# The up product of a conv FFN layer: sums of the right operand in place, another order of its seven products

## The chip, the cores and the metric

The kernel runs on one core of one Trainium2 chip, in float32. The metric is the device time of one execution in microseconds (us); of the kernel before there are three runs. Everything below about its inside comes from one profiled execution of it.

## The reference, cut to what matters

One layer of a diffusion transformer: adaptive modulation, a gated linear attention mixer beside a short convolution, the mixer's output product, a residual, and a conv FFN. The change touches the output product, the norm behind it and the FFN's first product (the up product):

```python
x = x + gt1 * rmsnorm(yx @ w_out, g_post_mix)          # 1024 tokens x 1024
hx = modulate(rmsnorm(x, g_pre_ffn), sh2, sc2)
u, gate = split(hx @ w_up, 2, axis=-1)                 # w_up: 1024 x 5632
u = dwconv_grid(u, w_cf, b_cf, 16, 64)                 # 3x3 taps on a grid of 16 x 64 tokens
x = x + gt2 * rmsnorm((silu(u) * gate) @ w_down, g_post_ffn)
```

All results are float32. The FFN has 2816 features, 22 tiles of 128; a pair `p` is one tile of u and the gate tile that belongs to it.

## The kernel before

**Products.** Each float32 operand is split into a high and a low part (`split`, L127 on ScalarE for the high part, L134 mostly on VectorE or GpSimd for the low), and a product is three matmuls: high by high, high by low, low by high (`mm3`, L144 to L146), each 128 x 128 by 128 x 512.

**The up product** is done by a scheme of Strassen's kind. For a pair, its four products of halves (u and gate, tokens 0 to 511 and 512 to 1023, over two halves of the 1024 inputs) become seven products m = 1 to 7. Each is 4 K tiles of 3 matmuls, so 12 matmuls into a PSUM bank of 128 x 512. Its left operand is a block of the pair's weights or a sum of blocks (`up_sum`; the sums run on GpSimd, L1161, into tiles `rs`), split by ScalarE and GpSimd into tiles `p`. Its right operand is a block of the normed tokens or a sum of blocks. Two right operands (tiles `b11` and `d0`) are made token tile by token tile in `norm2`; the others (`mx`) are made by `mixed` after the mixer's output product: sums `ms` over blocks `blk` at L1193, then splits.

**Banks.** The generator `pair` yields the next product, its bank, and whether it accumulates on what stands there. The order is 3, 4, 5, 1, 2, 7, 6 with banks bx, by, bx, bz, by, bz, bw. Where a bank is used twice, VectorE or ScalarE reads the value of the first product out, and the second accumulates on it. VectorE's six reads per pair are L1320, L1323, L1326, L1329, L1331 and L1337 (for the pairs ahead: L1308, L1311, L1315, L1331, L1337). Between the reads VectorE works on the 3x3 taps of the pair before (`conv`, L1260, one operation of 1.2 us per tap) and on sums of the gated features for the down product (L1279 to L1287).

**The pairs ahead.** For pairs 0 to 3 two of the seven products (4 and 2) run early (`early_prep`, `early_dot`): their right operands need only the first half of the tokens, so TensorE does them while the last token tile is normed.

**What sets the order.** TensorE's order is written out in the program throughout. The order on VectorE, ScalarE and GpSimd is that of the program from the transition on (`ordered`); ahead of it, and on SyncE (SP), which issues the loads and stores, a scheduler sets it. At `AHEAD = 3` products ahead, `load_up` and `prep_up` load and split the weights.

**The mixer's output product** runs over eight token tiles c (`w_out`), each with two halves of 512 columns; `half_stats` and `residual` norm a tile's result, and `norm2(c - 1)` transposes the token tile before, on TensorE, into `blk`. Tile 7's `norm2` comes after the early products of pairs 0 and 1. Its inputs are spilled earlier and loaded by SP: `so` (L1015), the gate's activations `sog` (L1018), the token rows x (L1020).

## Time and profile before

| what | value |
|---|---|
| median of 3 runs | 1190.06 us (1187.59 to 1190.59) |
| the profiled execution | 1189.29 us |
| its span | 1187.5 us |
| mean granted clock of TensorE | 0.989 |
| matmuls by the page | 5770, busy 1149.9 us (97%) |
| VectorE / ScalarE / GpSimd busy | 77% / 45% / 43% |

The span is what the profile records from the first to the last instruction. A row of the timeline gives start, duration, engine, line, operation, result<-inputs; in brackets the idle time ahead of the operation and what released it. A row of the groups gives the count, busy time, mean ns of one, and idle time before. A row of the windows gives the length, then busy time and count for TensorE, its weight loads, VectorE, ScalarE and GpSimd, then the granted clock as a share of full speed, the DMA engines' share, and GB/s. The mixing product's end, the transition and the up product lie at about 424 to 524, 524 to 570 and 570 to 985 us; then the down product follows.

### The profile page before, as it was taken

How to read it: one execution, taken by the hardware profiler on the slowest of the kernel's cores; microseconds unless marked ns; L12 is line 12 of the kernel's file. 1: busy time of each engine (PE TensorE's matmuls, PEld its weight loads, DVE VectorE, ACT ScalarE, POOL GpSimd, SP SyncE). 2: the span in 40 equal slices, each digit the busy share in tenths (PEclk: the TensorE clock that was granted, in tenths of full speed). 3: DMA queues.
4: the chain of work that ended last, by engine and by line, in shares of the span. 5: the costliest groups of instructions: out<-in, count | busy, mean ns of one | idle time of the engine just before them, and what ended most of it. 6: DMA issues, size and time to landing. Idle time of an engine off the chain costs nothing.

```text
span 1187.5 us, 15973 instructions
## 1 busy us (share of the span) xinstructions
PE 1149.9 (97%) x5770; PEld 945.9 (80%) x5770; DVE 910.0 (77%) x1237; ACT 531.4 (45%) x945; POOL 506.4 (43%) x415
## 2 busy tenths in 40 slices
PE   8899999979999999997999999999999999999997
PEld 6689977867877888885788888888888888888885
DVE  4965657898779456658689998888888887877676
ACT  5745156634243155555334434343434344544453
POOL 3111001233344201147888888787888872000002
PEclk9999999999999999999999999999999999999999
DMA  9883844401112273232213341233213249977663
GB/s 338 274 306 132 284 147 126 142 28 45 54 36 72 73 248 125 88 107 71 71 63 116 143 142 64 96 124 116 92 69 124 98 155 328 356 248 257 224 222 132
DMA packets 80128, 176.19 MB, mean 148 GB/s; under 512 B 9809, under 2 KB 21585, under 8 KB 80050
## 3 DMA queue, kind: packets, MB, share of 16 engines
q1 hardware_dynamic: 80050, 175.19, 43.7%
q8 instruction: 45, 0.74, 0.3%
q14 instruction: 33, 0.27, 0.1%
HBM read 142.38 MB, written 32.78 MB: 148 GB/s over the span
## 4 chain that ended last, share of the span: by engine, by line
PE 68%; DVE 12%; issue 7%; DMA 6%; POOL 3%; ACT 3%; SPq 0%; DVEq 0%; POOLq 0%; ACTq 0%
PE ps L144 21%; PE ps L146 21%; PE ps L145 21%; DMA ada<-in_ada 4%; DVE ada L229 3%; PE ps L889 2%; DVE su L852 2%; PE ps L334 1%; DVE p L134 1%; POOL rs L1161 1%; POOL ms L1193 1%; PE ps L923 1%; PE ps L922 1%; DVE mx L134 1%; DVE hxl L350 1%
## 5 line engine op out<-in xcount | busy, mean ns | idle before, releaser
L1260 DVE SCALAR_TENSOR_TENSOR y<-u,cols,y 128x945 f32<-128x945 f32 (+2 forms) x176 | 214.9, 1222 | 2.4
L144 PE MATMUL ps<-mx,p 128*128 128x512 f32 x440 | 174.5, 397 | 8.0 <-DVE t L1308 5.5
L145 PE MATMUL ps<-mx,p 128*128 128x512 f32 x440 | 174.6, 397 | 0.0
L146 PE MATMUL ps<-mx,p 128*128 128x512 f32 x440 | 174.2, 396 | 0.0
L134 POOL TENSOR_TENSOR p<-rs,p 128x512 fp32r<-128x512 f32 x106 | 138.2, 1306 | 39.8 <-ACT p L127 39.7
L146 PE MATMUL ps<-p,p 128*128 128x512 f32 x308 | 120.1, 390 | 0.2
L145 PE MATMUL ps<-p,p 128*128 128x512 f32 x308 | 120.1, 390 | 0.0
L144 PE MATMUL ps<-p,p 128*128 128x512 f32 x308 | 119.8, 389 | 0.0
L1161 POOL TENSOR_TENSOR rs<-wr 128x512 f32<-128x512 f32 x77 | 109.6, 1424 | 2.0 <-DMA wr<-in_wu 2.0
L134 POOL TENSOR_TENSOR wl<-wr,wh 128x1024 fp32r<-128x1024 f32 x16 | 41.4, 2593 | 158.9 <-ACT wh L127 158.9
L144 PEld LDWEIGHTS ps<-mx,p 128*128 128x128 f32 x440 | 83.6, 190 | 29.2 <-issue 7.0
L144 PE MATMUL ps<-hxh,wh 128*128 128x512 f32 x256 | 106.6, 416 | 0.0
L229 DVE CUSTOM_DVE_ANT_0 ada<-ada,cb 128x1024 f32<-128x1024 f32 x64 | 80.8, 1277 | 26.0 <-DMA ada<-in_ada 25.6
L146 PE MATMUL ps<-hxh,wl 128*128 128x512 f32 x256 | 100.6, 393 | 0.0
L145 PE MATMUL ps<-hxl,wh 128*128 128x512 f32 x256 | 100.2, 392 | 0.0
L145 PEld LDWEIGHTS ps<-mx,p 128*128 128x128 f32 x440 | 83.5, 190 | 19.1
L146 PEld LDWEIGHTS ps<-mx,p 128*128 128x128 f32 x440 | 83.5, 190 | 19.0
L127 ACT ACTIVATE p<-rs 128x512 fp32r<-128x512 f32 x110 | 68.5, 627 | 33.3 <-POOL rs L1161 32.9
L876 POOL TENSOR_TENSOR ek<-ek,kh 128x1024 f32<-128x1024 f32 x12 | 29.7, 2478 | 92.2 <-ACT ek L127 92.2
L145 PEld LDWEIGHTS ps<-p,p 128*128 128x128 f32 x308 | 57.8, 188 | 12.7 <-DVE p L134 0.7
L146 PEld LDWEIGHTS ps<-p,p 128*128 128x128 f32 x308 | 57.8, 188 | 12.7 <-DVE p L134 0.8
L144 PEld LDWEIGHTS ps<-p,p 128*128 128x128 f32 x308 | 57.8, 188 | 12.0
(282 smaller groups left out, 2678.2 us busy)
## 6 DMA issues: line engine op xcount, KB each, us to landing
ada<-in_ada SPq DMA_DIRECT2D x64, 512.0 KB, 4.5
wr<-in_wu SPq DMA_DIRECT2D x48, 512.0 KB, 4.4
h<-hd SPq DMA_DIRECT2D x77, 256.0 KB, 4.5
hd<-h SPq DMA_DIRECT2D x73, 256.0 KB, 2.1
wdr<-in_wd SPq DMA_DIRECT2D x55, 256.0 KB, 3.6
wdr<-in_wd SPq DMA_DIRECT2D x22, 512.0 KB, 5.9
x<-in_x SPq DMA_DIRECT2D x16, 512.0 KB, 5.1
wr<-in_wb SPq DMA_DIRECT2D x16, 512.0 KB, 3.7
```

The source lines that it names most:

```text
L127: return S.activation(o, i, fn, **kw)
L134: (eng or V).tensor_tensor(lo, raw, hi.bitcast(F32), ALU.subtract)
L144: PE.matmul(ps, lh, rh, start=first, stop=False, skip_group_check=more)
L145: PE.matmul(ps, lh, rl, start=False, stop=False, skip_group_check=more)
L146: PE.matmul(ps, ll, rh, start=False, stop=last, skip_group_check=more)
L229: V.tensor_tensor_reduce(raw, raw, cbs[which], 1.0, 0.0, ALU.mult, ALU.add, dst)
L334: PE.matmul(pt[:, j * P : (j + 1) * P], xs[t][:, ft * P : (ft + 1) * P], dgs[t], start=True, stop=True)
L852: V.scalar_tensor_tensor(slot(n)[lo : lo + DK, hs], slot(c)[lo : lo + DK, hs], dec[lo : lo + DK, h, c : c + 1], slot(n)[lo : lo + DK, hs], ...
L876: G.tensor_tensor(kl, kl, kh[hf], ALU.mult)
L889: PE.matmul(pts[hh][:, o : o + P], kl[r, fb, cs], ql[r, fb, cs], start=True, stop=True)
L1161: G.tensor_tensor(r, src[0], src[1], ALU.add if terms[1] > 0 else ALU.subtract)
L1260: V.scalar_tensor_tensor(y3[:, ro, co], u3[:, ri, ci], col("wcf", 9 * p + 3 * (dr_ + 1) + dc + 1), y3[:, ro, co], ALU.mult, ALU.add)
```

## The change

The right operands' sums are made in place, one token tile at a time. `norm2` returns four VectorE operations (128 x 512 each, L1086 to L1089 of the changed kernel) for a token tile of the second half; they write into `blk` and a tile `t7`. `mixed` now only splits. Rows of the first half make the tiles `b11` and `b21`. Four GpSimd row sums per pair remain of five, since one result serves the next.

The order of products becomes 1, 2, 6, 7, 4, 5, 3 (ahead: 6, 7, 4, 5, 3), with banks bx, by, bx, bz, bz, bw, bw. VectorE reads a bank five times per pair (L1319 or, ahead, L1312, then L1330, L1332, L1335 and L1337), ScalarE twice. The early products are 1 and 2, and tile 7's `norm2` stands between 1 and 2 of pair 1. The last token tile's output product goes K tile by K tile over both halves: five K tiles, then `norm2(6)`, then the rest. The order written out on VectorE, ScalarE and GpSimd begins with the last token tile. gv2 is loaded at the start of the down product, gv1 lies in a buffer of the output weights, and a constant (`tri`) moves to another pool.

```diff
-        b11, d0 = ([ph.tile([P, KQ, 512], F32R, name=f"{n}{i}") for i in range(2)] for n in ("b11", "d0"))
+        b11, b21 = ([ph.tile([P, KQ, 512], F32R, name=f"{n}{i}") for i in range(2)] for n in ("b11", "b21"))
...
+            x11, x12, x21, x22 = (blk[g][h][:, :, cs] for g in range(2) for h in range(2))
             if th == 0:
-                x0, x1 = (blk[g][0][:, :, cs] for g in range(2))
-                split(x0, b11[0][:, :, cs], b11[1][:, :, cs], heng=V)
-                raw = p2.tile([P, KQ, P], F32, tag="fd", bufs=1, name=nm("fd"))
-                fold(d0[0][:, :, cs], d0[1][:, :, cs], raw, x1, -1, x0, V, V, V)
...
+                split(x11, b11[0][:, :, cs], b11[1][:, :, cs], heng=V)
+                split(x21, b21[0][:, :, cs], b21[1][:, :, cs])
             else:
-                w_out(mh, ml, py, (0,), range(8))
-                if c < NT - 1:
-                    mix = mix_prep(c + 1)
-                w_out(mh, ml, py, (1,), range(5))
-                norm2(c - 1, *last)
-                xn, ss = norm_tiles()
-                half_stats(py, 0, xn, ss)
-                w_out(mh, ml, py, (1,), range(5, 8))
-            half_stats(py, 1, xn, ss)
-            normed = residual(c, xt, xn, ss)
-
-
-
-
-
-        pclose("pw")
-        pclose("pvo")
-        pc = popen("pc", "left", bufs=1)
-        py = popen("py", "left", bufs=1)
-
-        h_d = {m: [dr.tile([P, 512], F32, name=f"hd{m}_{i}") for i in range(KH)] for m in range(1, 8)}
-        FACT = {
-            1: (((0, 0), 1, (1, 1)), ((0, 0), 1, (1, 1))),
-            2: (((0, 1), 1, (1, 1)), ((0, 0),)),
-            3: (((0, 0),), ((0, 1), -1, (1, 1))),
-            4: (((1, 1),), ((1, 0), -1, (0, 0))),
-            5: (((0, 0), 1, (1, 0)), ((1, 1),)),
-            6: (((0, 1), -1, (0, 0)), ((0, 0), 1, (0, 1))),
-            7: (((1, 0), -1, (1, 1)), ((1, 0), 1, (1, 1))),
-        }
-
-
-        def up_raw(p, gate_only=False):
-            if gate_only or POS[p] % 2 == 0:
-                r = [None if gate_only and n == 0 else wp.tile([P, KT, P], F32, tag="wraw", name=nm("wr")) for n in range(2)]
+                d = t7[:, :, cs]
+                return [lambda: V.tensor_tensor(d, x22, x12, ALU.subtract),
+                        lambda: V.tensor_tensor(x12, x12, x11, ALU.subtract),
+                        lambda: V.tensor_tensor(x11, x11, d, ALU.add),
+                        lambda: V.tensor_tensor(x21, x21, x11, ALU.subtract)]
...
+        right = {6: blk[0][0], 7: t7, 4: blk[1][0], 5: blk[0][1], 3: blk[1][1]}
+        mixes = {}
+
+        def mixed(m, cols):
+
+            if m not in mixes:
+                mixes[m] = room("mx", pr, tag="mx", bufs=4) if m == 3 else room("mx", pa, tag="a")
+                rhs[m] = lambda kt: tuple(x[kt // 2][:, kt % 2, :] for x in mixes[m])
+            for g in range(2):
+                split(right[m][:, 2 * g : 2 * g + 2, cols], *(x[g][:, :, cols] for x in mixes[m]))
...
+        def up_sum(p, m, raw, free=True):
+            def row_sum(a, b, sign, r=None):
+                if r is None:
+                    r = pc.tile([P, KQ, P], F32, tag="rs", bufs=3, name=nm("rs"))
+                G.tensor_tensor(r, a, b, ALU.add if sign > 0 else ALU.subtract)
+                return r
+
+            a11, a12, a21, a22 = (r[:, KQ * h : KQ * h + KQ, :] for r in (raw[0], raw[-1]) for h in range(2))
+            if m == 6:
+                sums_of[p] = s7 = row_sum(a11, a21, -1)
+                sums_of[p] = s7, row_sum(a22, s7, -1)
+            return free, {1: lambda: a11, 2: lambda: a12, 4: lambda: a22, 5: lambda: row_sum(a21, a22, 1),
+                          6: lambda: sums_of[p][1], 7: lambda: sums_of[p][0],
+                          3: lambda: row_sum(a12, sums_of[p][1], -1, sums_of[p][1])}[m]()
...
+            elif c == NT - 1:
+                w_out(mh, ml, py, (0, 1), range(5))
+                early_prep(0)
+                sums = norm2(c - 1, *last)
+                mixed(6, c2)
+                mixed(7, c2)
+                w_out(mh, ml, py, (0, 1), range(5, 6))
+                w_out(mh, ml, py, (0,), range(6, 8))
+                xn, ss = norm_tiles()
+                half_stats(py, 0, xn, ss)
+                w_out(mh, ml, py, (1,), range(6, 8))
...
-        def mixed(m, hi, lo, cols, stage):
-            terms = FACT[m][1]
-            for g in range(2):
-                src = [blk[kh][th][:, 2 * g : 2 * g + 2, cols] for kh, th in terms[::2]]
-                h, l = hi[g][:, :, cols], lo[g][:, :, cols]
-                raw = src[0]
-                if len(src) > 1:
...
-                    raw = sums_of[m, g][:, :, cols]
-                if stage == 0:
-                    (G if m == 7 or m == 6 and g else V).tensor_tensor(raw, src[0], src[1],
-                                                            ALU.add if terms[1] > 0 else ALU.subtract)
-                elif stage == 1:
-                    split(raw, h, l)
...
-        UP, UP_AHEAD = (3, 4, 5, 1, 2, 7, 6), (3, 1, 5, 7, 6)
+        UP, UP_AHEAD = (1, 2, 6, 7, 4, 5, 3), (6, 7, 4, 5, 3)
...
             bx = bank(ps_mm)
-            yield 3, bx, False
-            if ahead:
-                V.tensor_tensor(t, g1, bx, ALU.add)
-                bz = bank(ps_mm)
-                yield 1, bz, False
-                V.tensor_tensor(g1, t, bz, ALU.add)
-                G.tensor_tensor(g1, g1, g0, ALU.subtract)
-                yield 5, bx, True
+            if p in kept:
+                u = kept[p].rearrange("p a b -> p (a b)")
+                yield 6, bx, False
+                V.tensor_tensor(u[:, hi], u[:, hi], bx, ALU.add)
+            else:
+                yield 1, bx, False
+                u = pc.tile([P, T], F32, tag="u", bufs=2, name=nm("u"))
                 act(u[:, hi], bx)
-                V.tensor_tensor(u[:, lo], t, bx, ALU.subtract)
+                by = bank(ps_mm)
+                yield 2, by, False
+                V.tensor_tensor(u[:, lo], u[:, hi], by, ALU.add)
+                yield 6, bx, True
+                act(u[:, hi], bx)
+            bz = bank(ps_mm)
+            yield 7, bz, False
+            if p == SEQ[-1]:
+                g = py.tile([P, T], F32, tag="y", bufs=3, name=nm("g"))
+            elif POS[p] % 2:
+                g = ph.tile([P, 2, T], F32, tag="blk", bufs=4, name=nm("g"))[:, 0, :]
             else:
-                act(t, bx)
-                by = bank(ps_mm)
-                yield 4, by, False
-                V.tensor_tensor(t, t, by, ALU.add)
-                yield 5, bx, True
-                act(u[:, hi], bx)
-                V.tensor_tensor(u[:, lo], t, bx, ALU.subtract)
-                bz = bank(ps_mm)
-                yield 1, bz, False
-                V.tensor_tensor(g1, t, bz, ALU.add)
-                yield 2, by, True
-                act(g0, by)
-                V.tensor_tensor(g1, g1, by, ALU.subtract)
-            yield 7, bz, True
-            V.tensor_tensor(u[:, lo], u[:, lo], bz, ALU.add)
+                g = pr.tile([P, T], F32, tag="g", bufs=2, name=nm("g"))
+            V.tensor_tensor(g[:, hi], u[:, hi], bz, ALU.add)
+            yield 4, bz, True
+            V.tensor_tensor(g[:, lo], u[:, hi], bz, ALU.add)
+            bw = bank(ps_mm)
+            yield 5, bw, False
+            V.tensor_tensor(g[:, hi], g[:, hi], bw, ALU.add)
+            yield 3, bw, True
+            V.tensor_tensor(u[:, hi], u[:, hi], bw, ALU.add)
             y = pools["yy"][1].tile([P, T], F32, tag="yy", bufs=2, name=nm("y"))
-            later.append(lambda: act(y, u, AF.Identity, bias=col("bcf", p), scale=col("wcf", 9 * p + 4)))
-            started.append(conv(p, u, y, g.rearrange("p a b -> p (a b)")))
-            bw = bank(ps_mm)
-            yield 6, bw, False
-            V.tensor_tensor(g1, g1, bw, ALU.add)
+            act(y, u, AF.Identity, bias=col("bcf", p), scale=col("wcf", 9 * p + 4))
+            started.append(conv(p, u, y, g))
...
-        early_prep(0)
         early_prep(1)
-        mixes = {m: room("mx", pa, tag="a") for m in MIXES[:4]}
-        c3, c1, call = slice(0, 3 * P), slice(3 * P, 4 * P), slice(0, 4 * P)
-        mixed(3, *mixes[3], c3, 0)
+        mixed(4, c2)
+        mixed(6, c6)
+        mixed(7, c6)
+        early_dot(0)
+        early_dot(1, lambda: [f() for f in norm2(NT - 1, *normed)])
+        mixed(6, c1)
         early_prep(2)
-        mixed(5, *mixes[5], c3, 1)
-        mixed(3, *mixes[3], c3, 1)
-        mixed(7, *mixes[7], c3, 0)
-        mixed(1, *mixes[1], c3, 0)
-        early_dot(0)
-        early_dot(1)
-        norm2(NT - 1, *normed)
+        keep(0)
+        mixed(7, c1)
         pclose("p2")
         pr = popen("pr", "right", bufs=1)
-        mixes[6] = room("mx", pr, tag="mx", bufs=4)
-        mixed(3, *mixes[3], c1, 0)
-        mixed(1, *mixes[1], c1, 0)
-        mixed(7, *mixes[7], c1, 0)
-        mixed(3, *mixes[3], c1, 1)
-        keep(0)
         early_prep(3)
-        mixed(1, *mixes[1], call, 1)
         early_dot(2)
+        keep(1)
+        mixed(4, c6)
         early_dot(3)
         load_up(0)
         prep_up(0)
         gen = pair(0)
         step = next(gen)
-        keep(1)
+        mixed(4, c1)
         load_up(1)
         prep_up(1)
-        mixed(5, *mixes[5], c1, 1)
+        mixed(5, slice(0, 512))
         load_up(2)
         prep_up(2)
-        mixed(6, *mixes[6], call, 0)
-        mixed(7, *mixes[7], call, 1)
+        mixed(3, slice(0, 512))
         load_up(3)
...
+        gv2 = pd.tile([P, D], F32, name="gv2")
+        SY.dma_start(gv2, gv2_row)
```

TensorE in a steady pair before: the last matmuls of product 2 and the first of product 7, which accumulates on product 1. In a row `ps` is a PSUM bank, `mx` or `b` the right operand, `p` the weights; brackets hold the semaphores waited for.

```order
L144 MATMUL ps_6003<-b_3825,p_6006 128x512
L145 MATMUL ps_6003<-b_3826,p_6006 128x512
L146 MATMUL ps_6003<-b_3825,p_6006 128x512
L144 MATMUL ps_6049<-mx_4852,p_6027 128x512 [waits DVE_49,Activation_49]
L145 MATMUL ps_6049<-mx_4854,p_6027 128x512
L146 MATMUL ps_6049<-mx_4852,p_6027 128x512 [waits Pool_49]
```

Product 1 lies in ps_6049, and the twelve matmuls of product 2 in ps_6003 stand between it and product 7. After, the end of product 7 and the start of product 4:

```order
L144 MATMUL ps_5986<-mx_4704,p_5907 128x512
L145 MATMUL ps_5986<-mx_4706,p_5907 128x512
L146 MATMUL ps_5986<-mx_4704,p_5907 128x512
L144 MATMUL ps_5986<-mx_4844,p_5948 128x512 [waits DVE_49]
L145 MATMUL ps_5986<-mx_4846,p_5948 128x512
L146 MATMUL ps_5986<-mx_4844,p_5948 128x512 [waits Pool_49]
```

Product 4 follows in the same bank ps_5986 as product 7, and its first matmul waits for VectorE. The same holds where 3 follows 5:

```order
L144 MATMUL ps_6033<-mx_5044,p_5967 128x512
L145 MATMUL ps_6033<-mx_5046,p_5967 128x512
L146 MATMUL ps_6033<-mx_5044,p_5967 128x512
L144 MATMUL ps_6033<-mx_5054,p_5991 128x512 [waits DVE_49,Activation_49]
L145 MATMUL ps_6033<-mx_5056,p_5991 128x512
L146 MATMUL ps_6033<-mx_5054,p_5991 128x512 [waits Pool_49]
```

VectorE over a steady pair before, from the read of product 4 to that of product 7:

```order
L1320 TENSOR_TENSOR t_5712<-t_5712,ps_5735 128x512
L1267 TENSOR_TENSOR h_5774<-y_5577,g_5443 128x1024
L1260 SCALAR_TENSOR_TENSOR y_5687<-u_5603,cols,y_5687 128x16x63
L1323 TENSOR_TENSOR u_5713<-t_5712,ps_5714 128x512
L1260 SCALAR_TENSOR_TENSOR y_5687<-u_5603,cols,y_5687 128x16x63
L1326 TENSOR_TENSOR g_5711<-t_5712,ps_5781 128x512
L1279 TENSOR_TENSOR h_5622<-h_5622 128x512
L1260 SCALAR_TENSOR_TENSOR y_5687<-u_5603,cols,y_5687 128x15x63
L1329 TENSOR_TENSOR g_5711<-g_5711,ps_5735 128x512
L1260 SCALAR_TENSOR_TENSOR y_5687<-u_5603,cols,y_5687 128x960
L1260 SCALAR_TENSOR_TENSOR y_5687<-u_5603,cols,y_5687 128x15x63
L1331 TENSOR_TENSOR u_5713<-u_5713,ps_5781 128x512
```

and after, from the read of product 2 (L1319) to that of 5 (L1335):

```order
L1319 TENSOR_TENSOR u_6386<-u_6386,ps_6388 128x512
L1275 SCALAR_TENSOR_TENSOR y_6367<-u_6237,cols,y_6367 128x960
L1275 SCALAR_TENSOR_TENSOR y_6367<-u_6237,cols,y_6367 128x15x63
L1275 SCALAR_TENSOR_TENSOR y_6367<-u_6237,cols,y_6367 128x16x63
L1330 TENSOR_TENSOR g_6449<-u_6386,ps_6430 128x512
L1302 TENSOR_TENSOR h_6257<-h_6257 128x512
L1275 SCALAR_TENSOR_TENSOR y_6367<-u_6237,cols,y_6367 128x16x63
L1275 SCALAR_TENSOR_TENSOR y_6367<-u_6237,cols,y_6367 128x15x63
L1332 TENSOR_TENSOR g_6449<-u_6386,ps_6430 128x512
L1275 SCALAR_TENSOR_TENSOR y_6367<-u_6237,cols,y_6367 128x960
L1335 TENSOR_TENSOR g_6449<-g_6449,ps_6471 128x512
```

Three taps stand between the reads of 2 and 7 (L1319 and L1330); between those of 7 and 5 (L1330 and L1335) the read of 4, three taps and a sum.

SP at the start of the mixing product, before:

```order
L693 DMA ogd_1664<-sc_3779 128x4x128
L705 DMA wor_3864<-in_wo 128x1024
L1018 DMA sog_3880<-ogd_1664 128x512
L1015 DMA so_3933<-scd_1666 128x512
L705 DMA wor_3870<-in_wo 128x1024
L693 DMA ogd_1665<-sc_3807 128x4x128
L1018 DMA sog_3937<-ogd_1664 128x512
L1015 DMA so_4020<-scd_1666 128x512
L1137 DMA wr_4820<-in_wu 128x1024
L1018 DMA sog_4024<-ogd_1664 128x512
```

and after:

```order
L705 DMA wor_3866<-in_wo 128x1024
L693 DMA ogd_1665<-sc_3807 128x4x128
L1014 DMA so_4015<-scd_1666 128x512
L1118 DMA wr_4669<-in_wu 128x1024
L1017 DMA sog_3877<-ogd_1664 128x512
L1019 DMA x_3879<-in_x 128x1024
L1017 DMA sog_3933<-ogd_1664 128x512
```

The first load of up weights (`wr`) stood behind the first two loads of `sog`; after, it stands ahead of both, and so does the store into ogd_1665.

More of the change, by code (lines that the diff above doesn't have):

```diff
@@ L974, in build @@
         pclose("pkq")
-        pgv = popen("pgv", "right", bufs=1)
-        gv2 = pgv.tile([P, D], F32, name="gv2")
         ph = popen("ph", "right", bufs=1)
@@ L1132, in up_raw @@
+        def up_raw(p, u_only=False):
+            if u_only and p > 1:
+                r = [pools["pc"][1].tile([P, KT, P], F32, tag="u", bufs=2, name=nm("wr"))]
+            elif u_only or POS[p] % 2 == 0:
+                r = [wp.tile([P, KT, P], F32, tag="wraw", name=nm("wr")) for n in range(1 if u_only else 2)]
             else:
@@ L1134, in up_raw @@
                 r = [t[:, 0], t[:, 1]]
[L1135 to L1137 removed]
+            for n in range(len(r)):
+                SY.dma_start(r[n], ap["wu"][2 * p + n])
             return r
@@ L1171, in up_product @@
+        pclose("pw")
+        pclose("pvo")
+        pc = popen("pc", "left", bufs=1)
+        py = popen("py", "left", bufs=1)
+        h_d = {m: [dr.tile([P, 512], F32, name=f"hd{m}_{i}") for i in range(KH)] for m in range(1, 8)}
         def up_product(m, a, pb, more=False):
@@ L1213, in keep, with early_dot @@
             act(kept[p][:, 1, :], early[p][0])
             V.tensor_tensor(kept[p][:, 0, :], kept[p][:, 1, :], early[p][1], ALU.add)
-        def early_dot(p):
+        def early_dot(p, between=None):
             pbs = [bank((ps_mm, ps_mm, ps_ms, ps_at)[p]) for _ in range(2)]
-            for m, a, pb in zip((4, 2), early[p], pbs):
+            for m, a, pb in zip((1, 2), early[p], pbs):
                 up_product(m, a, pb)
+                if m == 1 and between is not None:
+                    between()
@@ L1245, in light @@
             yield
-            while now[0] not in (2, 6, None):
+            while now[0] not in (4, 3, None):
                 yield
@@ L1555, in build @@
         now[0] = None
-        assert not later
         go_conv()
```

140 lines of the change are left out of this document (65 added, 75 removed).

## The prediction

> **What bounds the kernel now.** I read the page first (busy time, slices), then a table by windows, then TensorE's waits, and last the timeline around each read of a PSUM bank. The profiled execution took 1189.3 us for a span of 1187.5; the median shown is 1190.1, so a result on the profile's scale lies 0.8 below the median's.
>
> ```profile
> PE 1149.9 (97%) x5770; PEld 945.9 (80%) x5770; DVE 910.0 (77%) x1237; ACT 531.4 (45%) x945; POOL 506.4 (43%) x415
> PE   8899999979999999997999999999999999999997
> ...
> 570.00:985.00 415.00, 415.00 (x1789) 336.49 (x1788) 358.20 (x365) 166.24 (x257) 344.26 (x263) 1.00 0.31 107
> 550.00:575.00 25.00, 16.98 (x58) 13.06 (x57) 16.97 (x13) 10.35 (x17) 20.48 (x14) 0.80 0.13 43
> ...
> PE ps L144 <- DVE t L1308: 5.5, 1, 5.5
> PE ps L144 <- DVE g L1311: 2.5, 1, 2.5
> PE ps L146 <- DVE p L134: 1.3, 1, 1.3
> PE ps L1071 <- POOL dg L1055: 1.2, 1, 1.2
> ```
>
> TensorE bounds it. In the up product (about 570 to 985) it is busy for 415.00 of 415.00 us at full clock; its matmuls follow each other every 415.00 / 1789 = 0.232 us (a few records may be missing). No VectorE, ScalarE or GpSimd work saved there can shorten it, and every pause of TensorE is added in full. The only four waits between 525 and 990 belong to the transition from the mixing product: 10.5 us. Slow clock adds to it: in 550 to 575, 58 matmuls of 0.232 us would need 13.4 us and took 25, so 11.6 are lost where the two long waits are 8.0; 3.6 is the lowered clock. Transition now: 11.6 + 1.3 + 1.2 = 14.0 us.
>
> **The change part by part.**
>
> *Matmuls.* Seven products of 12 matmuls per pair stay, and the right operands lie half old tiles, half new. No matmul goes; 0.
>
> *Saved work.* Per pair one GpSimd row sum, one VectorE and one ScalarE bank read go; no group of wide right sums is left. All of it lies in the 415.00 of 415.00 stretch or under the transition's waits: 0 in the first, and in the second part of the term on the transition below. The cover is TensorE's own work; it would only fail if VectorE (358.20 of 415 busy) came to be late.
>
> *Two products into one bank, back to back.* Before, product 1 goes to bank bz, 2 to by, then 7 to bz again: always 12 matmuls of another bank lie between the end of a product and the next product that accumulates on it, and VectorE reads the bank under them. After, 4 follows 7 into the same bank, and 3 follows 5. VectorE has to read the intermediate value first (g from 7, g from 5), so the first matmul of 4 or 3 must wait until that read is over: twice in each of 22 pairs (ahead or not), 44 places. The price comes from these rows:
>
> ```profile
> 573.74 0.40 PE L146 MATMUL ps<-mx,p 128*128 128x512 f32 x1
> 574.18 0.69 DVE L1331 TENSOR_TENSOR u<-u,ps 128x512 f32<-128x512 f32 x1 [3.56 <-PE ps L146]
> ...
> 804.76 0.39 PE L146 MATMUL ps<-mx,p 128*128 128x512 f32 x1
> 804.99 0.40 PE L144 MATMUL ps<-b,p 128*128 128x512 f32 x1
> 805.26 0.69 DVE L1326 TENSOR_TENSOR g<-t,ps 128x512 f32<-128x512 f32 x1 [0.36 <-PE ps L146]
> ...
> 568.75 0.68 DVE L1311 TENSOR_TENSOR g<-t,ps 128x512 f32<-128x512 f32 x1
> 569.57 0.57 PE L144 MATMUL ps<-mx,p 128*128 128x512 f32 x1 [2.52 <-DVE g L1311]
> ...
> 545.69 0.50 PE L146 MATMUL ps<-d,p 128*128 128x512 f32 x1 [1.30 <-DVE p L134]
> 546.03 0.40 PE L144 MATMUL ps<-d,p 128*128 128x512 f32 x1
> 546.26 0.40 PE L145 MATMUL ps<-d,p 128*128 128x512 f32 x1
> ...
> L1331 DVE TENSOR_TENSOR u<-u,ps 128x512 f32<-128x512 f32 x22 | 15.0, 683 | 4.3 <-PE ps L146 4.3
> ```
>
> The read starts 574.18 - 573.74 = 0.44 us after the last matmul of its product starts (0.50 at 805.26); it lasts 0.68 (22 of them, 683 ns); TensorE goes on 569.57 - 569.43 = 0.14 after a read has ended. So 0.44 + 0.68 + 0.14 = 1.26 us pass from start to start where 0.23 did: 1.03. The first matmul after a wait costs 546.03 - 545.69 = 0.34 instead of 0.23: another 0.11. That is 1.14 for each place, 44 x 1.14 = 50 us. From below: without that restart and with a release of 0.05, 0.92, 44 times 40. From above: 0.50 for the start, 1.20, and in half of the places a filter tap ahead of the read:
>
> ```profile
> L1260 DVE SCALAR_TENSOR_TENSOR y<-u,cols,y 128x945 f32<-128x945 f32 x88 | 105.4, 1201 | 1.6
> L1260 DVE SCALAR_TENSOR_TENSOR y<-u,cols,y 128x1008 f32<-128x1008 f32 x44 | 55.8, 1268 | 0.1
> L1260 DVE SCALAR_TENSOR_TENSOR y<-u,cols,y 128x960 f32<-128x960 f32 x44 | 53.6, 1219 | 0.7
> L1279 DVE TENSOR_TENSOR h<-h 128x512 f32<-128x512 f32 x11 | 10.6, 967 | 0.0
> L1284 DVE TENSOR_TENSOR h<-h,h 128x512 f32<-128x512 f32 x10 | 16.7, 1667 | 0.3
> ```
>
> The order of VectorE puts, between the read of 2 and that of 7, three taps or fewer: 0.68 + 1.22 + 1.20 + 1.27 = 4.4 us, while TensorE takes 24 x 0.232 = 5.6. Between the reads of 7 and of 5 it puts at most 0.68 + 0.97 + 1.27 + 1.20 + 0.68 + 1.22 = 6.0, while 24 matmuls and a stall take 6.7. Both fit, the second with 0.7 to spare, so I take VectorE as ready: 1.14. If each second place were late by half a tap (0.6), 13 us come on top, and if all were, 26: the upper end is 53 + 26 = 79.
>
> The Trainium skill, "PSUM — Partial Sum Buffer" (Summary: rules for kernel authors), says that who reads PSUM while a matmul runs should aim the matmul at a different bank, guarded by bank. The order before keeps to this and shows no wait; the order after can't at these 44 places, and by that rule, too, the sum would be the full wait.
>
> *The transition.* The sums in place need 4 VectorE passes per token tile and most run under the mixing product, so the mx work behind the waits of 5.5 and 2.5 is smaller. New covers are thinner. The last token tile's norm now stands between product 1 and 2 of pair 1, with 12 matmuls (2.8 us) before pair 2's early products, where 48 stood. Behind that norm come:
>
> ```profile
> 537.45 2.91 ACT L127 ACTIVATE blk<-ps,sh,a 128x128 f32<-128x128 f32 x8 [1.41 <-PE ps L1071]
> 538.42 5.34 DVE L1193 TENSOR_TENSOR ms<-blk,blk 128x768 f32<-128x768 f32 x6
> 541.15 0.42 ACT L127 ACTIVATE mx<-ms 128x256 fp32r<-128x256 f32 x1 [0.79 <-DVE ms L1193]
> 543.35 0.62 ACT L127 ACTIVATE p<-rs 128x512 fp32r<-128x512 f32 x1
> 545.56 0.68 DVE L134 TENSOR_TENSOR p<-rs,p 128x512 fp32r<-128x512 f32 x1
> ```
>
> ScalarE's eight passes 2.9, of which VectorE's four sums (5.34 / 6 x 512 / 768 = 0.59 each) overlap about half, then the mx split ahead in ScalarE's queue (0.8 for two) and the weight split (0.62 + 0.68): 2.9 + 1.2 + 0.8 + 1.3 = 6.2, 3.4 after the cover. I add 1.7 for the norm of tile 6, which is issued 9 matmuls (2.0 us) sooner, 1.3 for the split ahead of pair 1 (the like of the 1.3 above) and 1.7 of lowered clock behind the longest wait: 8 instead of 14, so -6. Bounds: all 14 saved, or 3 lost if the chain behind the norm is again as late as 5.5 + 2.5 with more clock.
>
> *The start of the mixing product.* The scheduler put two loads of SP in another order: the first weight load of the early products (L1118 after) stands ahead of the load of the gate's activations (sog).
>
> ```profile
> 423.95 0.32 SPq L1018 DMA_DIRECT2D sog<-ogd  x1
> 427.84 0.47 SPq L1137 DMA_DIRECT2D wr<-in_wu  x1
> 427.97 1.28 ACT L127 ACT_TABLE_LOAD   x1 [0.82 <-DMA sog<-ogd]
> 429.93 0.75 DVE L1026 SCALAR_TENSOR_TENSOR sog<-ps,cols,sog 128x512 f32<-128x512 f32 x1 [1.52 <-ACT sog L127]
> 432.03 0.69 DVE L134 TENSOR_TENSOR ml<-sog,mh 128x512 fp32r<-128x512 f32 x1
> 432.77 0.50 PE L146 MATMUL ps<-woh,ml 128*128 128x512 f32 x1 [0.40 <-DVE ml L134]
> ```
>
> The sog load goes out at 423.95; ScalarE waits for it until 427.97, and the chain table load, silu, VectorE, split ends at TensorE, which waits 0.4. After, it stands behind the weight load, so it goes out near 427.8, 3.9 later; on VectorE a second sog operation (0.75) now stands ahead of the split, but a weight split of before no longer does. So TensorE waits about 3.5 more, and with some 1.7 of lowered clock I take +5. From below 0 (the load would be back in time), from above +8 (VectorE's queue on top).
>
> *Down stage and end.* gv2 is loaded (512 KB) where the down stage begins and used at the end: 0.
>
> Sum: 50 - 6 + 5 = +49. 1189.3 + 49 = 1238.
>
> **The rivals.** (a) The clock falls at each stall. Rows for it: at 569.57, after 2.52 us, matmuls stand 0.43 apart for eight:
>
> ```profile
> 569.94 0.63 PE L145 MATMUL ps<-mx,p 128*128 128x512 f32 x1
> ...
> 572.50 0.63 PE L145 MATMUL ps<-mx,p 128*128 128x512 f32 x1
> 572.93 0.52 PE L146 MATMUL ps<-mx,p 128*128 128x512 f32 x1
> ```
>
> Eight times 0.20 is 1.6, 44 times 70: 1308. Against it: after the wait of 1.30 the next two matmuls came 0.34 and 0.23 apart, full speed. The Trainium skill, "TensorE: Matmul & The Clock Gate" (A second HAM failure mode: psum-queue depth-cycling), tells of short idles between groups of matmuls that made the clock swing; it is this rival, and the row at 546.03 speaks against it for one idle, not for 44. Chance 0.05. (b) VectorE is late at half the places or more: +13 to +26, 1251 to 1264; 0.12. (c) Only one of the two stalls per pair binds, or the price is nearer its floor: 22 x 1.14 = 25 to 40, 1213 to 1228; 0.10. (d) The other side: the wait is over when TensorE comes to it, and only the transition counts. The point from which it decides: if the transition gave back all of its 14 us, 44 places must cost under 0.32 us each. But 0.44 + 0.14 - 0.23 = 0.35 pass even with a read of no length, so the read would have to overlap the matmuls still streaming. Then 1189.3 - 6 to - 14: 1175 to 1183. Chance 0.05. (e) The waits are there, but cost little more than 0.32, and all terms cancel: 0.02.
>
> **How the numbers follow.** The forecast (1229 to 1251: 44 stalls of 1.0 to 1.25, other terms within their bounds) has 0.66; with (a) 0.05, (b) 0.12, (c) 0.10, (d) 0.05, (e) 0.02. The range takes in most of (b) and (c): 1220 to 1260 leaves out (a), (d), (e) and the tails, about 0.18. Faster by over 0.3%, which is about what a measurement of this kernel can tell from no change: (d), 0.05; within it: 0.02; slower: 0.93.
>
> **What would show it.** In the changed profile: 44 waits of TensorE for VectorE at the lines of 7's and 5's reads (L1330, L1335), each near 1.0 us; no window of the up product filled by TensorE, with 22 x 1.14 x 2 us spread evenly; the clock column at 1.00 there; a wait near 3 to 4 us where the mixing product starts and another before pair 2. The prediction is wrong if the up product's windows are still full, if the reads start later than 0.5 us after the last matmul, or if matmuls after a stall stand 0.43 apart.

## The result

The changed kernel takes 1241.85 us (median of 4 runs, 1240.66 to 1245.47) against 1190.32 for the kernel before on the same chips; the ratio is 1.0439, 95% interval 1.0407 to 1.047. The forecast was 1238, with 1220 to 1260 around it. The profiled execution has a span of 1239.7 us, 52.2 more than before.

The lines of its page that answer to those shown of before, then the table by windows, and TensorE's waits from 424 us on (in a row of waits: total us, times, longest):

```profile
PE 1160.9 (94%) x5770; PEld 942.8 (76%) x5770; DVE 876.4 (71%) x1218; ACT 521.4 (42%) x935; POOL 455.8 (37%) x384
PE   7999999979999979989899999998999999999997
PEclk9999999989999989999999999999999999999999
...
570.00:1040.00 470.00, 430.90 (x1820) 338.26 (x1819) 337.55 (x351) 156.90 (x242) 316.31 (x244) 1.00 0.29 99
...
PE ps L144 <- DVE g L1330: 20.0, 22, 1.4
PE ps L144 <- DVE g L1335: 18.3, 21, 0.9
PE ps L144 <- ACT mh L127: 6.6, 1, 6.6
PE ps L144 <- ACT p L127: 3.9, 2, 3.4
PE ps L1073 <- DVE xn L1056: 1.3, 1, 1.3
```

The matmuls are the same 5770. From 570 us on TensorE was filled for 415.00 of 415.00 us; now 39 of 470 us are idle there, in waits of about 0.9 us, at full clock. (Both windows reach past the up product: the first matmul of the down product starts at 968.60 us before and at 1021.21 after. 43 of the 44 expected waits are in the two upper rows; the other, of 0.83 us at 579.87, is there without a releaser.) VectorE, ScalarE and GpSimd all have less to do than before, and none of it shows in the time.

Where the 52.2 us went, by the starts of the same matmuls in both traces (first of the mixer's output product, first early product, first product of the pairs' loop, first of the down product, end):

| stretch | before | after | difference |
|---|---|---|---|
| ahead of the mixer's output product | 425.76 | 427.41 | +1.65 |
| output product | 97.93 | 107.87 | +9.94 |
| early products | 27.26 | 31.01 | +3.75 |
| the loop over pairs | 417.65 | 454.92 | +37.27 |
| down product and end | 218.90 | 218.49 | -0.41 |

The loop before held the transition's two long waits and the lowered clock behind them, 11.6 us by the prediction's estimate. Without these the loop grew by 37.27 + 11.6 = 48.9 us. Two of the 44 places in the changed kernel's timeline, first TensorE at both and then VectorE at the first:

```profile
902.19 0.39 PE L146 MATMUL ps<-mx,p 128*128 128x512 f32 x1
903.43 0.50 PE L144 MATMUL ps<-mx,p 128*128 128x512 f32 x1 [0.85 <-DVE g L1330]
903.76 0.39 PE L145 MATMUL ps<-mx,p 128*128 128x512 f32 x1
903.99 0.40 PE L146 MATMUL ps<-mx,p 128*128 128x512 f32 x1
...
908.88 0.39 PE L146 MATMUL ps<-mx,p 128*128 128x512 f32 x1
910.14 0.47 PE L144 MATMUL ps<-mx,p 128*128 128x512 f32 x1 [0.87 <-DVE g L1335]
...
902.69 0.69 DVE L1330 TENSOR_TENSOR g<-u,ps 128x512 f32<-128x512 f32 x1 [1.00 <-PE ps L146]
```

The last matmul of product 7 starts at 902.19, VectorE's read 0.50 later, it lasts 0.69, and product 4 starts 0.05 after its end: 1.24 us from start to start, where 0.23 would be, and 1.26 at the second place (908.88 to 910.14). The start after that of product 4 is 0.33 later, the one after that 0.23. VectorE stood idle for 1.00 us ahead of the read: it was ready, and the read could begin no sooner.

### The profile page after: what moved, and what is told of

It is laid out like the page before. It is cut to its first block, busy times and chain, and to the rows that moved or that the text cites. A ratio compares the mean times of both kernels' runs of the same rounds, so it can differ in the third digit from the quotient of the medians.

```text
span 1239.7 us, 15817 instructions
## 1 busy us (share of the span) xinstructions
PE 1160.9 (94%) x5770; PEld 942.8 (76%) x5770; DVE 876.4 (71%) x1218; ACT 521.4 (42%) x935; POOL 455.8 (37%) x384
## 4 chain that ended last, share of the span: by engine, by line
PE 46%; DVE 5%; issue 2%; ACT 1%; DMA 0%; DVEq 0%; POOL 0%; POOLq 0%; ACTq 0%
PE ps L144 16%; PE ps L146 15%; PE ps L145 15%; DVE g L1330 1%; DVE g L1335 1%; DVE p L134 1%; DMA hd<-h 0%; DVE y L1275 0%; ACT p L127 0%; DVE h L1297 0%; ACT jk L127 0%; DVE top L1475 0%; DVE top L1478 0%; ACT y L127 0%; DVE u L1337 0%
## 5 line engine op out<-in xcount | busy, mean ns | idle before, releaser
L144 PE MATMUL ps<-mx,p 128*128 128x512 f32 x440 | 176.6, 401 | 39.1 <-DVE g L1330 20.0
L134 POOL TENSOR_TENSOR p<-rs,p 128x512 fp32r<-128x512 f32 x88 | 114.5, 1304 | 150.4 <-ACT p L127 150.4
L144 PEld LDWEIGHTS ps<-mx,p 128*128 128x128 f32 x440 | 82.6, 188 | 74.2 <-issue 32.5
L229 DVE CUSTOM_DVE_ANT_0 ada<-ada,cb 128x1024 f32<-128x1024 f32 x64 | 79.8, 1260 | 32.2 <-DMA ada<-in_ada 32.1
L127 ACT ACTIVATE p<-rs 128x512 fp32r<-128x512 f32 x88 | 54.8, 626 | 109.6 <-POOL rs L1142 103.7
L146 PEld LDWEIGHTS ps<-mx,p 128*128 128x128 f32 x440 | 82.7, 188 | 18.8
L145 PEld LDWEIGHTS ps<-mx,p 128*128 128x128 f32 x440 | 82.7, 188 | 17.1
L127 ACT ACTIVATE y<-u,cols 128x1024 f32<-128x1024 f32 x22 | 26.6, 1210 | 145.2 <-DVE u L1337 145.2
L134 POOL TENSOR_TENSOR p<-wr,p 128x512 fp32r<-128x512 f32 x58 | 75.4, 1300 | 5.4 <-ACT p L127 5.4
L144 PE MATMUL ps<-b,p 128*128 128x512 f32 x176 | 70.4, 400 | 3.9 <-ACT p L127 3.9
L146 PE MATMUL ps<-b,p 128*128 128x512 f32 x176 | 70.1, 398 | 0.2 <-DVE p L134 0.2
L145 PE MATMUL ps<-b,p 128*128 128x512 f32 x176 | 70.2, 399 | 0.0
```

Source lines behind the costliest of these rows:

```text
L127: return S.activation(o, i, fn, **kw)
L134: (eng or V).tensor_tensor(lo, raw, hi.bitcast(F32), ALU.subtract)
L144: PE.matmul(ps, lh, rh, start=first, stop=False, skip_group_check=more)
L145: PE.matmul(ps, lh, rl, start=False, stop=False, skip_group_check=more)
L146: PE.matmul(ps, ll, rh, start=False, stop=last, skip_group_check=more)
L229: V.tensor_tensor_reduce(raw, raw, cbs[which], 1.0, 0.0, ALU.mult, ALU.add, dst)
```

## The experiments

The theory to be tested: a product that accumulates in the bank of the product right ahead of it, whose value VectorE must read out first, costs TensorE about 1.1 us at each place, and nothing else in the up product costs anything. The first rival: VectorE or the weights are late in the new order, and the waits only show it.

**Another product between the two.** The order 1, 2, 6, 7, 5, 4, 3 keeps everything of the change but puts 5 between 7 and 4, and 4 between 5 and 3:

```diff
-        UP, UP_AHEAD = (1, 2, 6, 7, 4, 5, 3), (6, 7, 4, 5, 3)
+        UP, UP_AHEAD = (1, 2, 6, 7, 5, 4, 3), (6, 7, 5, 4, 3)
...
             V.tensor_tensor(g[:, hi], u[:, hi], bz, ALU.add)
-            yield 4, bz, True
-            V.tensor_tensor(g[:, lo], u[:, hi], bz, ALU.add)
             bw = bank(ps_mm)
             yield 5, bw, False
             V.tensor_tensor(g[:, hi], g[:, hi], bw, ALU.add)
+            yield 4, bz, True
+            V.tensor_tensor(g[:, lo], u[:, hi], bz, ALU.add)
             yield 3, bw, True
...
```

(The sums of the gated features move from products 4 and 3 to 5 and 3, the same places in the order.)

> The changed kernel with products 5 and 4 exchanged (1, 2, 6, 7, 5, 4, 3): product 5 stands between 7 and 4, product 4 between 5 and 3, all else kept. Theory (each product that accumulates right behind the read of its own bank costs about 1.1 us, and nothing else in the up product costs anything): the 43 waits on L1330 and its like are gone, the up product is filled, about 48 us less than the changed kernel: 1194 us, some 4 above before, which is the start of the mixing product (6.6 us wait) less the transition's gain. Rival (VectorE or the weights are late in the new order, and the waits only show it): waits of TensorE stay, at other lines; over 1220 us.

Measured: 1193.89 us (10 runs), ratio to before 1.0037 (1.0019 to 1.0054). That is 48 us less than the changed kernel, as expected. From 570 to 985 us, and TensorE's waits from 535 to 1080:

```profile
570.00:985.00 415.00, 413.84 (x1784) 333.87 (x1783) 335.91 (x345) 153.43 (x240) 314.97 (x239) 1.00 0.32 107
...
PE ps L144 <- ACT p L127: 3.8, 2, 3.2
PE ps L144 <- DVE g L1333: 0.7, 1, 0.7
```

One short wait of 44 is left and the stretch is filled again. The rival falls: with the same work and the same number of taps between the reads, VectorE and the weights are in time. The loop over the pairs lasts 408.11 us here, against 454.92 in the changed kernel: 46.8 us, or 1.06 for each of 44 places, without any estimate of what the transition took.

**One of the two adjacent places.** The order 1, 2, 6, 5, 7, 4, 3 puts 5 into its bank first, then 7, right behind it 4, and then 3:

```diff
-        UP, UP_AHEAD = (1, 2, 6, 7, 4, 5, 3), (6, 7, 4, 5, 3)
+        UP, UP_AHEAD = (1, 2, 6, 5, 7, 4, 3), (6, 5, 7, 4, 3)
...
-            while now[0] not in (4, 3, None):
+            while now[0] not in (7, 3, None):
...
```

The second pair of lines says at which products VectorE makes the sums of the gated features; here they move to 7 and 3.

> The changed kernel in the order 1, 2, 6, 5, 7, 4, 3: 4 still follows 7 into one bank, but 3 no longer follows 5. Theory (price per place, the places add up): half of the 44 waits, about 24 us less than the changed kernel: 1218 us. Rival (one long stall per pair, or a common cause of both waits): no less than half of the loss goes or stays whole: 1194 or 1242 us.

Measured: 1260.75 us, ratio 1.0598 (1.0569 to 1.0626), more than with both places. Neither side of the expectation held. One place of this run, VectorE's rows and then TensorE's:

```profile
803.56 0.86 DVE L1294 TENSOR_TENSOR h<-h 128x512 f32<-128x512 f32 x1
804.34 2.50 DVE L1275 SCALAR_TENSOR_TENSOR y<-u,cols,y 128x1008 f32<-128x1008 f32 x2
806.75 0.68 DVE L1334 TENSOR_TENSOR g<-g,ps 128x512 f32<-128x512 f32 x1
...
805.23 0.39 PE L146 MATMUL ps<-mx,p 128*128 128x512 f32 x1
807.58 0.47 PE L144 MATMUL ps<-mx,p 128*128 128x512 f32 x1 [1.97 <-ACT p L127]
...
808.83 0.56 PE L146 MATMUL ps<-mx,p 128*128 128x512 f32 x1
809.18 0.63 PE L144 MATMUL ps<-mx,p 128*128 128x512 f32 x1
...
811.74 0.63 PE L144 MATMUL ps<-mx,p 128*128 128x512 f32 x1
812.17 0.48 PE L145 MATMUL ps<-mx,p 128*128 128x512 f32 x1
...
570.00:985.00 415.00, 376.38 (x1535) 298.99 (x1534) 282.68 (x297) 128.30 (x199) 266.24 (x207) 0.95 0.26 89
```

In this order a sum and two taps stand on VectorE ahead of the read that TensorE waits for. The bank was ready about 805.7 (the start of the last matmul and the 0.5 us of the rows above), the read began at 806.75 and ended at 807.43; TensorE went on 0.15 later. (The row names ScalarE's weight split as releaser, which ended at about the same time. In all 22 places of the trace TensorE starts 0.15 us after the end of VectorE's read, also in the six where no weight split ended within 0.9 us of that start; so it is the read. That is what to check when a wait has several semaphores.) The wait is 2.0 us instead of 0.9, and some matmuls after it run at half speed: at 809.18 to 811.74 they start 0.43 apart. So it goes behind 13 of the 22 waits. The granted clock over the stretch is 0.95.

**The same order with VectorE free.** Whether the price comes from the order of the products or from what stands ahead of the read is told apart by moving VectorE's work alone (the edit against the run before):

```diff
-        TAPS = (1, 2, 1, 2, 1, 1)
+        TAPS = (1, 2, 2, 1, 1, 1)
...
-            while now[0] not in (7, 3, None):
+            while now[0] not in (4, 3, None):
```

> The run with order 1, 2, 6, 5, 7, 4, 3 again, with VectorE's work dealt out anew so that only one tap (1.2 us) and no sum stands ahead of the read of 7 (taps 1, 2, 2, 1, 1, 1; sums at products 4 and 3). The first time VectorE had two taps and a sum there, the wait was 2.1 us, and the clock fell to 0.95. Theory (the price of a place is the read alone as long as VectorE is free, and grows with what stands ahead of the read): 22 waits of 0.9 us, clock 1.00, 24 us more than with no stall: 1218 us. Rival (accumulating 4 right behind 7 costs over 2 us in this order, whatever VectorE does): 1260 us again.

Measured: 1220.69 us, ratio 1.0263 (1.0242 to 1.0283).

```profile
PE ps L144 <- DVE g L1334: 22.4, 22, 2.7
...
570.00:985.00 415.00, 393.50 (x1675) 313.83 (x1674) 310.84 (x324) 140.22 (x217) 290.76 (x225) 1.00 0.28 95
```

Twenty-two waits, 1.0 us on average (18 of them 0.87 to 0.92), the clock back at 1.00. Against the order without adjacent products that is 1220.69 - 1193.89 = 26.8, or 1.22 for a place: the price adds up by places, and 40 us between this run and the one before came from VectorE's order alone.

**A longer read.** The same VectorE operation, twice, ahead of product 4 (the result is the same):

```diff
             V.tensor_tensor(g[:, hi], u[:, hi], bz, ALU.add)
+            V.tensor_tensor(g[:, hi], u[:, hi], bz, ALU.add)
             yield 4, bz, True
```

> The changed kernel, VectorE's read of product 7 done twice (the same operation again, the same result), so that product 4 waits for two reads. Theory (TensorE waits for VectorE's read and goes on at its end): the waits at this place grow by the pitch of such a read, 0.60 us, the others stay: 22 x 0.60 = 13 us more, 1255 us. Rival (the wait is a fixed turnaround of the bank or the semaphore, the read lies beside it): 1242 us. Rival (VectorE has no room, so that the second kind of read gets late too): more than 13 us.

Measured: 1257.81 us, ratio 1.0571 (1.0541 to 1.0601): 16.0 more than the changed kernel. VectorE's two reads, TensorE's next matmul, and the waits:

```profile
691.21 0.68 DVE L1330 TENSOR_TENSOR g<-u,ps 128x512 f32<-128x512 f32 x1
691.93 0.69 DVE L1331 TENSOR_TENSOR g<-u,ps 128x512 f32<-128x512 f32 x1
...
692.76 0.47 PE L144 MATMUL ps<-mx,p 128*128 128x512 f32 x1 [1.69 <-DVE g L1331]
...
PE ps L144 <- DVE g L1331: 35.8, 21, 2.1
PE ps L144 <- DVE g L1336: 18.3, 21, 0.9
```

The two reads start 0.72 apart, not the 0.60 I had put in, and 22 x 0.72 = 15.8. The waits at this place grew from 0.91 to 1.70, those at the other stayed 0.87. So TensorE waits for the end of the read, and the fixed turnaround is excluded; so is the third view, that the second kind of read gets late, though the time alone (more than 13 us) would have fitted it.

**The adjacency alone, in the kernel before.** Products 1 and 2 exchanged in the 18 pairs that run all seven; nothing of the change:

```diff
-        UP, UP_AHEAD = (3, 4, 5, 1, 2, 7, 6), (3, 1, 5, 7, 6)
+        UP, UP_AHEAD = (3, 4, 5, 2, 1, 7, 6), (3, 1, 5, 7, 6)
...
-            while now[0] not in (2, 6, None):
+            while now[0] not in (1, 6, None):
...
```

> The kernel before, with products 1 and 2 exchanged in its 18 pairs that run all seven (3, 4, 5, 2, 1, 7, 6): product 7 then follows product 1 into the same bank. Nothing else of the change. Theory (the adjacency alone costs about 1.1 us a place): 18 waits, 20 us more than before: 1210 us. Rival (the waits need the change's other parts, such as VectorE's or GpSimd's new order): 1190 us.

Measured: 1253.22 us, ratio 1.0532 (1.0499 to 1.0565), three times what was expected. It is the miss of the second run again: my second line had moved a sum ahead of the awaited read. VectorE's rows and TensorE's:

```profile
815.57 1.80 DVE L1287 TENSOR_TENSOR h<-h 128x512 f32<-128x512 f32 x1
817.29 1.20 DVE L1260 SCALAR_TENSOR_TENSOR y<-u,cols,y 128x945 f32<-128x945 f32 x1
818.40 0.68 DVE L1329 TENSOR_TENSOR g<-g,ps 128x512 f32<-128x512 f32 x1
...
819.23 0.47 PE L144 MATMUL ps<-mx,p 128*128 128x512 f32 x1 [2.12 <-ACT p L127]
```

So that line was taken back, and the products' exchange kept:

> The kernel before with products 1 and 2 exchanged again, but with the sum that stood ahead of the read of product 1 on VectorE kept at product 2, as in the kernel before. With it the 18 waits were 2.1 us and the clock 0.95. Theory: 18 waits near 0.9 us, clock 1.00, 20 us over before: 1210 us. Rival: 1253 us again.

Measured: 1214.11 us, ratio 1.0213 (1.0186 to 1.024).

```profile
PE ps L144 <- DVE g L1329: 20.5, 18, 1.2
...
817.85 1.20 DVE L1260 SCALAR_TENSOR_TENSOR y<-u,cols,y 128x945 f32<-128x945 f32 x1
818.96 0.68 DVE L1329 TENSOR_TENSOR g<-g,ps 128x512 f32<-128x512 f32 x1
819.78 0.47 PE L144 MATMUL ps<-mx,p 128*128 128x512 f32 x1 [1.17 <-DVE g L1329]
...
570.00:985.00 415.00, 395.68 (x1689) 316.36 (x1688) 345.49 (x345) 154.45 (x239) 314.46 (x248) 1.00 0.27 96
```

Eighteen waits of 1.14 us and 1214.11 - 1189.23 = 24.9 us, 1.4 for a place, a little over the forecast: VectorE comes straight from a tap here, with no idle time ahead of the read, so the read begins 0.7 us after the last matmul's start (mean of the 18) and not 0.43 to 0.54 as in the changed kernel. The adjacency has its price without any other part of the change.

**The start of the mixing product.** With the stalls gone, the changed kernel was still 0.4% behind before, in spite of a shorter transition. The changed kernel's SP, ScalarE and TensorE there:

```profile
427.88 0.37 SPq L693 DMA_DIRECT2D ogd<-sc  x1
428.84 0.71 SPq L1118 DMA_DIRECT2D wr<-in_wu  x1
433.43 0.32 SPq L1017 DMA_DIRECT2D sog<-ogd  x1
...
436.75 1.28 ACT L127 ACT_TABLE_LOAD   x1 [3.09 <-DMA sog<-ogd]
...
440.18 0.80 PE L144 MATMUL ps<-woh,mh 128*128 128x512 f32 x1 [6.61 <-ACT mh L127]
445.46 0.51 PE L144 MATMUL ps<-woh,mh 128*128 128x512 f32 x1
```

The sog load goes out at 433.43 (423.95 before), and TensorE waits 6.61 us, then runs 12 matmuls at about 0.43 to 445.46. For the next run, on the order without adjacent products, SP's order is written out there: sog and the token rows of tiles 0 and 1, then gv1 (512 KB), then the first up weights.

```diff
+        loads = tc.manual_schedule(engines={mybir.EngineType.SP})
+        loads.__enter__()
         mix = mix_prep(0)
-        SY.dma_start(gv1, rows(16, "gp1"))
+        gv1_row = rows(16, "gp1")
         gv2_row = rows(40, "gp2")
...
                 mix = mix_prep(1)
+                SY.dma_start(gv1, gv1_row)
+                raw0 = up_raw(0, True)
+                loads.__exit__(None, None, None)
...
```

> The run without adjacent products (1, 2, 6, 7, 5, 4, 3), with the loads at the start of the mixing product issued in the program's order: sog ahead of gv1's 512 KB and of the first 512 KB of up weights. Theory (the 6.6 us wait there is the late sog load): the wait falls to about 2 us, the slow clock behind it goes, 5 to 6 us less: 1188 us. Rival (sog waits for the store of its tile, not for its place in the queue): no change, 1194 us.

Measured: 1194.76 us, ratio 1.0041 (1.0024 to 1.0058): no change. One of SP's waits there, then TensorE's rows, ScalarE's row on tile 1, and from the transfers the stores of the two rows for gv1 and gv2 (count, KB each, us to landing):

```profile
SPq L1017 <- DMA ogd<-sc: 3.4, 1, 3.4
...
434.50 0.80 PE L144 MATMUL ps<-woh,mh 128*128 128x512 f32 x1 [4.63 <-ACT mh L127]
444.80 0.50 PE L144 MATMUL ps<-woh,mh 128*128 128x512 f32 x1 [2.50 <-ACT mh L127]
...
444.12 0.63 ACT L127 ACTIVATE mh<-so 128x512 fp32r<-128x512 f32 x1 [9.68 <-DMA so<-scd]
...
row<-gv SPq DMA_DIRECT2D x2, 4.0 KB, 13.8
```

Both sides were partly right. The wait fell from 6.9 us (in the run without adjacent products) to 4.6; most of the rest is that sog waits 3.4 us for the store of ogd that now stands ahead of it in SP's order (in the kernel before, sog went out ahead of that store). And what was won came back ten us later: my order had put the stores of gv1's and gv2's rows, 4 KB each, ahead of tile 1's loads. They took 13.8 us to land, and so of tile 1, issued behind them at 430.05, landed at 444.04, just after them, and reached ScalarE only at 444.12.

**The early split.** The wait of 3.2 us before pair 2's early products, with their weight splits put ahead of the last token tile's norm:

```diff
-        early_dot(1, lambda: [f() for f in norm2(NT - 1, *normed)])
-        mixed(6, c1)
-        early_prep(2)
+        early_dot(1, lambda: (early_prep(2), [f() for f in norm2(NT - 1, *normed)]))
+        mixed(6, c1)
```

> As the run before, and the weight splits of pair 2's early products ahead of the last token tile's norm and sums on ScalarE and VectorE. Theory (the 3.2 us wait before these products is the split behind the sums): that wait goes, with some slow clock behind it: 4 us less than the run before, 1184 us. Rival (the wait moves on to the next thing that needs the norm): as the run before.

Measured: 1189.95 us, ratio 1.0004 (0.9993 to 1.0014); 4.8 us less than the run before it, where 4 were expected. The wait before pair 2 is gone (the longest wait for a weight split is 0.6).

**The rows first.** Last, the two small stores ahead of the ordered loads, on top of that:

```diff
-        loads = tc.manual_schedule(engines={mybir.EngineType.SP})
-        loads.__enter__()
-        mix = mix_prep(0)
         gv1_row = rows(16, "gp1")
         gv2_row = rows(40, "gp2")
+        loads = tc.manual_schedule(engines={mybir.EngineType.SP})
+        loads.__enter__()
+        mix = mix_prep(0)
```

> As the last run (no adjacent products, loads in order, early split), but the two small stores of gv1's and gv2's rows go ahead of the ordered loads. In the runs before it SP stood 9.1 us behind such a store (the load of gv1 waits for it), so that tile 1's load of so came late and TensorE waited 2.5 us more at 444.8. Theory: that wait goes, the wait at the start stays near 4.6 us: 1189.95 - 2.5 - some slow clock = 1186 us. Rival (SP then waits at another load, such as sog's for the store of ogd, and the wait at the start grows): 1190 us.

Measured: 1188.08 us (12 runs) against 1191.24 of before on the same chip, ratio 0.9978 (0.9966 to 0.999). Against before that is 3.9 us less than the last run, about what was expected. The 2.5 us wait is gone, that at the start stays; the two stores now go out at 152.61 and 215.42 us. The expectation named SP's queue as what held tile 1 up; by the rows of the run before it was rather the landing of a load issued in time; this run shows only that the wait goes when the stores go.

```profile
PE ps L144 <- ACT mh L127: 4.7, 1, 4.7
PE ps L144 <- DVE g L1338: 1.3, 2, 0.8
PE ps L1073 <- DVE xn L1056: 1.3, 1, 1.3
PE ps L144 <- ACT u L127: 1.2, 1, 1.2
```

So the change's parts without its adjacent products, with its loads in order and the early split, come out slightly ahead of the kernel before, by 0.1 to 0.3%. The 4.7 us at the start are left; bringing sog ahead of the store of ogd was not tried.

## Why the prediction was right, step by step

- **TensorE bounds the up product, and saved work on the others is worth nothing there.** Right. VectorE's work went from 910 to 876 us and GpSimd's from 506 to 456; with the adjacent products taken apart the stretch is as filled as before (413.84 of 415.00), and its loop of 408.11 us is no shorter than that of before without the 11.6 (406.05).
- **Forty-four stalls of 1.14 us, 50 us.** Right: 44 waits stand in the profile, 39.1 us of idle time, and the loop grew by 48.9, 1.11 for a place (46.8 and 1.06 against the run without adjacent products). From the start of the last matmul to that of the next it was 1.24 and 1.26 us at the two places shown, 1.26 by the prediction; where the read began 0.06 later than put in, TensorE went on that much sooner after it. The experiment that takes the adjacency away returned 48 us, the two that have it alone (in the kernel before, or at one place per pair) cost 1.2 to 1.4 for a place. The lower bound's 0.92 comes to 0.94 by its own rows; nothing hangs on it.
- **VectorE is ready.** Right for the change as written: it was idle ahead of the reads, 0.8 us on average, and the longest wait at the read of 5 is 0.9. The 0.7 us to spare that the prediction gave this read were worked out with the shorter of its two rows for a sum (0.97); the longer (1.67) would have left nothing, so the margin was less sure than it said. The step's price for the other case was too low. I had put a late read at 0.6 us and 13 to 26 us in all; the two runs in which a sum or a tap too many stood ahead of the read lost 1253.22 - 1214.11 = 39 and 1260.75 - 1220.69 = 40 us on 18 and 22 places, since waits of 2 us also lowered the clock.
- **Rival (a), the clock falls at each stall.** It did not: 1.00 over the loop, and 0.33 and 0.23 between the matmuls after a wait. By the Trainium skill, "TensorE: Matmul & The Clock Gate" (A second HAM failure mode: psum-queue depth-cycling), short idles between groups of matmuls can make the clock swing; here it held for waits of 0.9 to 1.7 us, and swung behind 13 of 22 waits of 2 us.
- **Rivals (c) to (e).** Both kinds of place bind, 22 times each, at 0.91 and 0.87 us of wait; and no read there overlaps a matmul.
- **The transition, -6.** Right: after, 1.3 us at the norm of tile 6 (1.7 were put in), 0.6 + 0.2 at pair 1's split (1.3), 3.4 before pair 2 (3.4), and the slow clock behind it. The output product's share of 1.3 and the early products' +3.75 against -11.6 make -6.5. The 11.6 is the prediction's own estimate: with the loop of the run without adjacent products as the measure, the stalls are 46.8 and the transition is -4.5. The traces fix the sum of the two, 42.3, better than its parts.
- **The start of the mixing product, +5 with 8 as the upper end.** The mechanism was right and the size off: 9.94 - 1.3 = 8.6, above my bound. The step that failed is "it stands behind the weight load, so it goes out near 427.8". It went out at 433.43, because the store of ogd had also moved ahead of it: issued at 427.88, among loads of the output weights and gv1, it landed at 433.35 (5.5 us, where the one at 422.43 took 2.3), and SP waited for that. I had read the order, and not followed what the load waits for. Why it waits is open: by SP's order as printed above that store goes into ogd_1665 and the load reads ogd_1664, and before, the load went out ahead of the store.
- **Down stage and end, 0.** Right (-0.41).
- **Not foreseen:** TensorE comes to the output product 1.65 us later. The profile has a wait of 1.3 us there (L795 for VectorE's L488) that the run without adjacent products, with the same code in that place, shows at 0.3. It is no more than the scatter between executions: the output product starts at 424.98 to 428.06 in the profiles of the four other runs with the changed kernel's code ahead of it, and at 424.68 and 428.13 in the two with that of before.

The sum of the terms as measured is 48.9 - 6.5 + 8.6 + 1.65 - 0.4 = 52.2; predicted was 49.

## What to carry to other kernels

A product that goes on in the bank of the one just finished, with a read between the two, costs TensorE the whole read with its latencies, here 1.1 us against 12 matmuls of 2.8 us; one other product in between costs nothing and needs only that the bank stays taken longer. So the order of products in a scheme with fewer sums is to be chosen by banks first. Where such a read can't be hidden, count what stands ahead of it on the reading engine: in two pairs of runs, one or two operations too many turned waits of 1.0 and 1.1 us into 2.0 and 2.1, and with the lowered clock a place cost 3.0 and 3.5 us.

## What the runs showed of the hardware that was not expected

- **Regular pauses and the granted clock.** In the up product's loops here, pauses of 0.9 us (44 of them) left the granted clock at 1.00, and so did 18 of 1.1 us and 22 of 1.7 us (with 22 of 0.9 between); with 22 of 2.0 us on average it was 0.95, and with 17 of 2.1 to 2.2 us too. Of the 22 pauses, 13 were followed by seven or eight matmuls 0.43 apart, which began 0.6 to 1.6 us after the pause, and nine by none; what tells them apart isn't shown.
- **Two reads of one bank in a row** into the same tile started 0.72 us apart on VectorE, where two reads of different banks into different tiles stood 0.60 apart (568.75 and 569.35 in the trace of before).
- **A store of 4 KB that takes 13.8 us.** A 256 KB load issued right behind the two stores of a transposed row (128 x 8 single values) took from 430 to 444 us to be used, where such loads landed in 4.5 us in the last run. The stores are as slow elsewhere: in the kernel before they go out at 153.62 and 218.47 us and take 11.3 and 11.1 us.
